# A streaming encoder step: rows of u at an even pace, ten single sets of v rows, and row requests three ahead

## The chip, the core and the metric

The kernel runs on one core of one Trainium2 chip. The metric is the device time of one execution in microseconds (us); the time before is the median of three runs. The engines are called as the profile calls them: PE (matmul), PEld (its weight load), DVE (vector), ACT (scalar), POOL (general purpose; it issues the gathers) and SP (it issues the weight transfers).

## The reference, cut to what matters

The model has two layers. Each ends in a PEER block: every token of the normed stream `xn` picks 128 experts (8 heads x 16) of 16,384, takes their rows `u` of a table (1,024 numbers each), multiplies them with its own `xn`, puts the sums through a gelu and a gate, and adds up the experts' rows `v` with these factors.

```python
eid = (e1 * PEER_NKEYS + e2).reshape(PEER_TOKEN_BLOCK, PEER_HEADS * PEER_TOPK)
ue = jnp.take(u_tab, eid, axis=0)
act = jax.nn.gelu(jnp.einsum('tkd,td->tk', ue, xb).astype(jnp.float32))
ve = jnp.take(v_tab, eid, axis=0)
return jnp.einsum('tk,tkd->td', (gate * act).astype(xb.dtype), ve)
```

There are 384 tokens: 256 of a prompt and 128 of running streams (the sample). All arithmetic is float32.

## The kernel before

The function `peer` (L924) does the block twice, once per layer. The prompt tokens are done densely: PE multiplies with the whole tables, 128 blocks of 128 experts each. The sample tokens are done sparsely, by gathered rows. Both run beside each other, and the sparse part is dealt out over the dense part by step numbers.

**Steps.** Steps 0 to 63 make the first half of the dense u products. Steps 64 to 127 (here the gates stage, loop at L1529) make the second half, and beside them the first half of the gates. Steps 128 to 255 (here the values stage, loop at L1564) multiply with the v blocks; up to about step 188 they also make the second half of the gates. A step of the values stage has on PE twelve matmuls (L179) or, in every fifth step of the first sixty, eight unsplit ones (L1436). The block arrives by SP as `raw` (512 KB); ACT makes `hi` (L130), DVE makes `lo` (L131) two steps before PE needs it, and DVE also makes `plo` of the activations. Every second step has a gate: DVE makes `ob`, `og` and half of `oa` (L1376 to L1394), PE takes them in sixteen short matmuls (L1403), DVE multiplies the result into `G` (L1409).

**Rows of u.** The 128 u rows of the sample are gathered by POOL (L1233), one row per partition, 128 x 1024 numbers, into a ring of three buffers `gath`, and DVE multiplies each with `xn` and sums it up (L1278, `u_item`). `U_DUE` (L61) gives how many rows shall be done before a step; between its pairs the rows are dealt out evenly (`tick`, L1450). The request for row k+2 stands in the program ahead of the product of row k. A request can go out when its buffer is free: with three buffers, when the product of row k-3 is done.

**Sets of v rows.** 96 of the 128 v rows are taken on PE in sets of four (`v_quad`, L1340, sixteen matmuls at L1348). `V_DUE` (L62) gives the step of each of the 24 sets: six in the gates stage, 18 in the values stage. In the values stage the rows lie in eight slots of `G[0]`, room for two sets, so the four gathers of a set wait until PE has taken the set two before it. The other 32 rows (`v_item`, L1298) are summed on DVE (L1303) in the steps between the two numbers of `I_DUE` (L59). The last gate is multiplied in at about step 188, and from step 192 on both halves of `G` are done with: the work on the sample fills what DVE has left. This last part of the values stage is what the title of the change calls phase 192.

**What sets the order.** PE, DVE and ACT keep the order in which the program is written through both stages (`in_order`, L85). POOL and SP do not: their order is the scheduler's. Each is a queue: a gather that waits holds back all gathers behind it. The extra buffers of the values stage (third `hi` and `lo`) lie in the pool `lpool` (L1558).

Of the kernel before, what the change touches and what calls it, by code (L numbers as in the profile page):

```python
# [9 lines left out]
F32 = mybir.dt.float32  # L10
F32R = mybir.dt.float32r
# [8 lines left out]
P = 128  # L20
D = 1024
KD = D // P
NB = 3
NP = 256
# [31 lines left out]

GD = 2
QR = [r for r in range(32) if r // RG != GD]
I_DUE = (192, 250)  # L59
AHEAD = 2 * 64 - 5  # L60
U_DUE = ((64, 22), (71, 27), (78, 33), (104, 53), (128, 72), (148, 87), (196, P))  # L61
V_DUE = ([82, 86, 90, 94, 98, 103] + [149 + 6 * i for i in range(7)] + [196 + 9 * (i // 2) for i in range(11)])  # L62
V_SLOTS = [(1, 36 + 4 * i, 66, 100 + 4 * i) for i in range(6)] + [(0, e, 128 + e + 5, 256) for e in (0, 4, 8, 12, 20, 24, 28, 32)]


# [1 line left out]
def encoder_step(ctx: ExitStack, tc: tile.TileContext, t_in, t_out):  # L67
# [4 lines left out]
    def T(pl, shape, dt=F32, tag=None, bufs=None):  # L72
        n_names[0] += 1
        return pl.tile(shape, dt, tag=tag, name=f"{tag}_{n_names[0]}", **({} if bufs is None else {"bufs": bufs}))
# [62 lines left out]
    more, turn_of = {}, {}  # L137
# [786 lines left out]
    def peer(l):  # L924
        with ExitStack() as c:
            one = c.enter_context(tc.tile_pool(name="p1", bufs=1))

            eidU = T(one, [P, GR, TG], I32, tag="eidU")
# [15 lines left out]
            gap = lambda n, i: T(qpool, [P, n // 4], F32, tag=f"gap{i}")  # L944
# [1 line left out]
            sync.dma_start(sk, t_in["sub_k"][l])  # L946
            gap(192, 0)
            qhi = T(qpool, [P, KD, NT], F32R, tag="qhi")
            gap(224, 1)
            qlo = T(qpool, [P, KD, NT], F32R, tag="qlo")  # L950
            gap(96, 2)
            qTp = T(qpool, [P, 2 * PH, NP], F32, tag="qTp")

            grow = G[0][:, HE - 4:].rearrange("p e t -> p (e t)")
# [6 lines left out]
            lpool = lent.__enter__()  # L961
# [268 lines left out]
            urows, vrows = {}, {}  # L1230

            def gather(tile_, tab, idx):
                pool.indirect_dma_start(out=tile_, out_offset=None, in_=tab,  # L1233
                                        in_offset=bass.IndirectOffsetOnAxis(ap=idx, axis=0))
                return tile_

            def fetch_u(k):
                if k < P:
                    g, j = divmod(k, TG)
                    urows[k] = gather(T(one, [P, D], F32, tag="gath", bufs=3), t_in["p_u"], eidU[:, g, j:j + 1])  # L1240

            def fetch_v(n, s):

# [6 lines left out]
            def v_slot(n, s):  # L1250
                return next((k for *k, s0, s1 in V_SLOTS if s0 <= s and V_DUE[n // 4] <= s1 and tuple(k) not in taken), None)

# [67 lines left out]
            def item_tick(s):  # L1320
                want = min(TG, max(0, TG * (s + 1 - I_DUE[0]) // (I_DUE[1] - I_DUE[0])))
                while done["i"] < want:
# [4 lines left out]
                    if done["i"] == TG:  # L1327
                        items_end()
                if s >= I_DUE[0] - 4:
                    fetch_item(s - 2 * HE)  # L1330
# [113 lines left out]
            done = {"u": 0, "v": 0, "f": 0, "i": 0, "g": 0, "c": 0}  # L1444
# [5 lines left out]
            def tick(s):  # L1450

                s0, n0 = start[0], 0
                for s1, n1 in U_DUE:
                    if s < s1:
                        break
                    s0, n0 = s1, n1
                want = P if s >= U_DUE[-1][0] else n0 + (n1 - n0) * (s + 1 - s0) // (s1 - s0)
                while done["u"] < want:
                    fetch_u(done["u"] + 2)
                    u_item(done["u"])  # L1460
                    done["u"] += 1

# [29 lines left out]
            for e2 in range(HE):  # L1492
                j = e2 - (HE - TURN)
                if j == 0:
                    more.clear()
                    lent.__exit__(None, None, None)
                    xfctx.__exit__(None, None, None)
                    xpool = tc.tile_pool(name="px", bufs=1, side="right")
                    xp = xpool.__enter__()
                    xhi = T(xp, [P, KD, NP], F32R, tag="xhi")  # L1500
                    T(xp, [P, 8], F32, tag="gap")
                    xlo = T(xp, [P, KD, NP], F32R, tag="xlo")
                u_gelu(e2, u_products(e2, u_weights(e2)))
                if j >= 0:
                    ks = slice(2 * (j // 2), 2 * (j // 2) + 2)
                    x_, q_ = ((xhi, qhi), (xlo, qlo))[j % 2]
                    pin(act.copy(x_[:, ks], q_[:, ks, :NP]))
                if busy:
                    busy = pull(sample, 2)
                    if not busy:  # L1510
                        start[0] = e2 + 1
                        fetch_u(0)
                        fetch_u(1)
                else:
                    pull(prompt, 2 if e2 % 4 == 0 else 1)
                    tick(e2)
# [41 lines left out]
            lpool = (lent := tc.tile_pool(name="pe1", bufs=1, side="right")).__enter__()  # L1558
            turn_of.pop("hi"), turn_of.pop("lo")
            turn_of.update(hi=1, lo=1)  # L1560
            more.update(hi=(lpool, 1), lo=(lpool, 1))
            stage = [(wt, ph)]
            n = 1
            for e2 in range(2 * HE):  # L1564
# [44 lines left out]
    peer(0)  # L1609
    attention()  # L1610
    peer(1)
    final()

# [95 lines left out]
```

## Time and profile before

| What | Value |
|---|---|
| runs | 2437.0, 2439.88, 2450.36 us; median 2439.88 |
| profiled execution | 2438.17 us; its span 2436.5 us |
| busy, share of the span | PE 96%, PEld 83%, DVE 81%, ACT 51%, POOL 31% |
| DMA | 649.76 MB, mean 267 GB/s |
| gates stage, layer 0 and 1 | 665.8 to 888.2 us and 1765.0 to 1991.1 us |
| values stage, layer 0 and 1 | 888.2 to about 1325 us and 1991.1 to about 2426 us |

The profile is of one execution. In a group of instructions the last column is the time that the engine stood idle just before them and what ended it. In the table by stretch of time each engine has its busy time in the stretch, so that the stretch less PE's busy time is PE's idle time; the columns behind POOL are the granted TensorE clock, the busy share of the DMA engines and GB/s. Step numbers are not in the trace: they are counted from the matmuls.

### The profile page before, as it was taken

To read this page: it belongs to the slowest core of one execution; us is meant where nothing else is said; L and a number is where in the kernel's file an instruction comes from. 1 tells how busy PE (TensorE), PEld (TensorE's weight loads), DVE (VectorE), ACT (ScalarE), POOL (GpSimd) and SP (SyncE) were. 2 spreads that over 40 slices of the span, in tenths; PEclk is the share of its full clock that TensorE was granted. 3 is DMA by queue.
4 is the path that set the end of the run, shared out by engine and by line. 5 is a ranking of instruction groups with operands and counts; after the bars stand their busy time and mean duration, and the time that the engine had idled before them with its cause. 6 is when DMAs were issued, how large, how long until landed. Compare 5 with 4: busy or idle time off the path is not lost.

```text
span 2436.5 us, 44422 instructions
## 1 busy us (share of the span) xinstructions
PE 2345.2 (96%) x16591; PEld 2011.4 (83%) x16592; DVE 1965.2 (81%) x4233; ACT 1249.7 (51%) x2428; POOL 747.7 (31%) x779
## 2 busy tenths in 40 slices
PE   7999999999999999899999998999999999999998
PEld 7899988999998987566776877999998997666776
DVE  5988846989998999787776675989997999787676
ACT  5656524434565666454444554344465666453443
POOL 2222200012245334455551100011244324454550
PEclk9999999999999999999999999999999999999999
DMA  5555434357799889999995424357799889999995
GB/s 198 176 187 179 155 134 159 136 211 247 254 336 365 307 299 335 354 381 352 415 393 170 139 71 166 126 212 250 247 343 340 308 298 332 372 374 349 413 400 182
DMA packets 177080, 649.76 MB, mean 267 GB/s; under 512 B 21136, under 2 KB 23040, under 8 KB 174208
## 3 DMA queue, kind: packets, MB, share of 16 engines
q1 hardware_dynamic: 99936, 365.85, 41.7%
q0 software_dynamic: 76928, 281.07, 31.1%
q8 instruction: 130, 2.13, 0.3%
q14 instruction: 86, 0.70, 0.1%
HBM read 630.62 MB, written 18.06 MB: 266 GB/s over the span
## 4 chain that ended last, share of the span: by engine, by line
PE 80%; DVE 7%; DMA 5%; issue 4%; ACT 3%; POOL 1%; another core or an unknown queue 0%; POOLq 0%; SPq 0%; ACTq 0%; DVEq 0%
PE bank L179 24%; PE bank L166 13%; PE bank L168 13%; PE bank L167 12%; DMA gath<-in_p_u,eidU 5%; PE bank L1348 3%; PE bank L1361 2%; PE bank L1403 2%; DVE lo L131 2%; PE bank L1436 2%; DVE gath L1278 1%; ACT hi L130 1%; PE bank L533 1%; PE bank L472 1%; PE bank L473 1%
## 5 line engine op out<-in xcount | busy, mean ns | idle before, releaser
L130 ACT CAST hi<-raw 128x1024 fp32r<-128x1024 f32 (+1 forms) x476 | 495.4, 1041 | 728.8 <-PE bank L167 324.2
L131 DVE TENSOR_TENSOR lo<-raw,hi 128x1024 fp32r<-128x1024 f32 (+1 forms) x476 | 575.7, 1210 | 193.8 <-ACT hi L130 166.2
L1233 POOL DMA_INDIRECT gath<-in_p_u,eidU x256 | 323.8, 1265 | 863.8 <-DVE gath L1278 516.8
L166 PE MATMUL bank<-xhi,hi 128*128 128x256 f32 (+1 forms) x1344 | 407.1, 303 | 0.9 <-issue 0.9
L168 PE MATMUL bank<-xhi,lo 128*128 128x256 f32 (+1 forms) x1344 | 398.0, 296 | 9.4 <-DVE lo L131 8.2
L167 PE MATMUL bank<-xlo,hi 128*128 128x256 f32 (+1 forms) x1344 | 398.4, 296 | 0.0
L168 PEld LDWEIGHTS bank<-xhi,lo 128*128 128x128 f32 x1344 | 255.2, 190 | 14.9 <-DVE lo L131 12.9
L166 PEld LDWEIGHTS bank<-xhi,hi 128*128 128x128 f32 x1344 | 253.9, 189 | 16.1 <-issue 8.7
L1233 POOL DMA_INDIRECT G<-in_p_v,eidT x192 | 213.7, 1113 | 141.1 <-PE bank L1348 76.1
L167 PEld LDWEIGHTS bank<-xlo,hi 128*128 128x128 f32 x1344 | 255.5, 190 | 0.4
L166 PE MATMUL bank<-qhi,hi 128*128 128x256 f32 (+1 forms) x784 | 232.9, 297 | 0.0
L168 PE MATMUL bank<-qhi,lo 128*128 128x256 f32 (+1 forms) x784 | 228.6, 292 | 2.0 <-DVE lo L131 2.0
L167 PE MATMUL bank<-qlo,hi 128*128 128x256 f32 (+1 forms) x784 | 229.6, 293 | 0.0
L179 PE MATMUL bank<-lo,phi 128*128 128x512 f32 x632 | 198.5, 395 | 9.2 <-DVE lo L131 9.0
L1391 ACT ACTIVATE oa<-ioh,e2T 128x128 f16<-128x128 f16 x512 | 163.3, 390 | 84.5 <-PE bank L1403 80.0
L179 PE MATMUL bank<-hi,phi 128*128 128x512 f32 x632 | 205.5, 406 | 0.2
L130 ACT CAST hix<-raw 128x1024 fp32r<-128x1024 f32 x118 | 123.7, 1048 | 152.1 <-PE bank L167 70.2
L179 PE MATMUL bank<-hi,plo 128*128 128x512 f32 x632 | 196.2, 392 | 0.0
L1278 DVE SCALAR_TENSOR_TENSOR gath<-gath,G 128x1024 f32<-128x1024 f32 x128 | 155.9, 1218 | 36.6 <-DMA gath<-in_p_u,eidU 33.2
L1278 DVE SCALAR_TENSOR_TENSOR gath<-gath,xg 128x1024 f32<-128x1024 f32 x128 | 155.5, 1216 | 9.2 <-DMA gath<-in_p_u,eidU 9.2
L131 DVE TENSOR_TENSOR lox<-raw,hix 128x1024 fp32r<-128x1024 f32 x118 | 143.7, 1218 | 22.2 <-ACT hix L130 19.2
L179 PEld LDWEIGHTS bank<-hi,phi 128*128 128x128 f32 x632 | 115.0, 189 | 44.2 <-issue 18.7
(391 smaller groups left out, 5120.9 us busy)
## 6 DMA issues: line engine op xcount, KB each, us to landing
raw<-in_u_t SPq DMA_DIRECT2D x256, 512.0 KB
raw<-in_p_v SPq DMA_DIRECT2D x256, 512.0 KB
raw<-in_w_in SPq DMA_DIRECT2D x32, 512.0 KB
raw<-in_p_w_q SPq DMA_DIRECT2D x32, 512.0 KB
raw<-in_w_z SPq DMA_DIRECT2D x16, 512.0 KB
s<-in_state_ssm SPq DMA_DIRECT2D x8, 1024.0 KB
out_sm_ssm<-s SPq DMA_DIRECT2D x8, 1024.0 KB
raw<-in_w_out SPq DMA_DIRECT2D x16, 512.0 KB
```

The source lines that it names most:

```text
L130: act.copy(hi, raw)
L131: dve.tensor_tensor(lo, raw, hi32, op=OP.subtract)
L166: pe.matmul(ps, whi[:, s], xhi[:, k, c0:c1], start=(k == 0), stop=False)
L167: pe.matmul(ps, whi[:, s], xlo[:, k, c0:c1], start=False, stop=False)
L168: pe.matmul(ps, wlo[:, s], xhi[:, k, c0:c1], start=False, stop=(k == KD - 1))
L179: mm = pe.matmul(ps, x, w[:, hf * n:(hf + 1) * n], start=s_, stop=e_)
L1233: pool.indirect_dma_start(out=tile_, out_offset=None, in_=tab, in_offset=bass.IndirectOffsetOnAxis(ap=idx, axis=0))
L1278: pin(dve.scalar_tensor_tensor(tile_, tile_, 1.0, xg[g], op0=OP.mult, op1=OP.mult, accum_out=au[g][:, j:j + 1]))
L1348: pe.matmul(out_s[hf][32 * q:32 * q + 32, :], cm[:, q], rows[q][:, hf * 512:hf * 512 + 512], start=(r == 0), stop=False, tile_position=(0, ...
L1361: pe.matmul(ps, wt[0][:, k * P:(k + 1) * P], xf[:, k], start=(k == 0), stop=(k == KD - 1))
L1391: act.activation(a[:, i], ioh, AF.Square, scale=-1.0, bias=e2T[:, t, 0:1])
L1403: pe.matmul(ps[:, i], ones[i // 4][:, i % 4], eg[:, i, j], start=(j == 0), stop=(j == 1))
```

## The change

Three tables and one buffer change; no arithmetic does.

- `U_DUE`: 46 rows in the gates stage (50 before), 47 in steps 128 to 191 (52 before), and the last 13 in steps 192 to 202, more than one a step. All 128 are done after step 202 (195 before).
- `V_DUE`: the sets six steps apart go on to step 203 (ten of them; seven before). The last eight come in pairs at 207, 218, 229 and 240. Before, eleven came from 196 to 241, in pairs nine steps apart but for the last.
- `I_DUE`: the 32 rows on DVE are dealt out over steps 203 to 249, not 192 to 249.
- In the values stage every fourth u row (k % 4 = 3) gets a buffer of its own, `gathx`, in `lpool`, and the request for row k+3 stands ahead of the product of row k. A request then waits for the product of row k-4. The gaps between `qhi`, `qlo`, `qTp` and between `xhi`, `xlo` are moved so that the pools still fit.

```diff
-I_DUE = (192, 250)
+I_DUE = (203, 250)
 AHEAD = 2 * 64 - 5
-U_DUE = ((64, 22), (71, 27), (78, 33), (104, 53), (128, 72), (148, 87), (196, P))
-V_DUE = ([82, 86, 90, 94, 98, 103] + [149 + 6 * i for i in range(7)] + [196 + 9 * (i // 2) for i in range(11)])
+U_DUE = ((64, 22), (128, 68), (192, 115), (203, P))
+V_DUE = ([82, 86, 90, 94, 98, 103] + [149 + 6 * i for i in range(10)] + [207 + 11 * (i // 2) for i in range(8)])
...
             qhi = T(qpool, [P, KD, NT], F32R, tag="qhi")
-            gap(224, 1)
             qlo = T(qpool, [P, KD, NT], F32R, tag="qlo")
-            gap(96, 2)
+            gap(64, 1)
             qTp = T(qpool, [P, 2 * PH, NP], F32, tag="qTp")
...
             def fetch_u(k):
                 if k < P:
                     g, j = divmod(k, TG)
-                    urows[k] = gather(T(one, [P, D], F32, tag="gath", bufs=3), t_in["p_u"], eidU[:, g, j:j + 1])
+                    extra = k % 4 == 3 and k >= more.get("u", P)
+                    tile_ = T(lpool, [P, D], F32, tag="gathx", bufs=1) if extra else T(one, [P, D], F32, tag="gath", bufs=3)
+                    urows[k] = gather(tile_, t_in["p_u"], eidU[:, g, j:j + 1])
...
                 while done["u"] < want:
-                    fetch_u(done["u"] + 2)
+                    fetch_u(done["u"] + 2 + ("u" in more))
                     u_item(done["u"])
...
                     xhi = T(xp, [P, KD, NP], F32R, tag="xhi")
+                    xlo = T(xp, [P, KD, NP], F32R, tag="xlo")
                     T(xp, [P, 8], F32, tag="gap")
-                    xlo = T(xp, [P, KD, NP], F32R, tag="xlo")
...
-            more.update(hi=(lpool, 1), lo=(lpool, 1))
+            more.update(hi=(lpool, 1), lo=(lpool, 1), u=done["u"] + 2)
+            fetch_u(more["u"])
```

What it does to the queues is seen at three places, all in layer 0 (layer 1 reads alike). The lines of kernel.py are one or two off between the two versions. The first is POOL's queue at the four gathers that wait for the set of step 185. In the names, `gath` and `gathx` are buffers of u rows, `eidT` stands in gathers for a set, `eidU` with `G` in gathers for DVE's rows. Before, the u row right behind the four (gath_13071, row 121) is due in step 188:

```order
L1233 DMA gath_13036<-in_p_u,eidU_3964 128x1024
L1233 DMA G_626_3975<-in_p_v,eidT_3971 128x1024 x4
L1233 DMA gath_13071<-in_p_u,eidU_3964 128x1024
L1233 DMA G_626_3975<-in_p_v,eidU_3964 128x1024
L1233 DMA gath_13110<-in_p_u,eidU_3964 128x1024
L1233 DMA gath_13153<-in_p_u,eidU_3964 128x1024
```

And now, where the row behind the same four is row 113 (gath_13045), due in step 190:

```order
L1232 DMA gath_13010<-in_p_u,eidU_3964 128x1024
L1232 DMA G_626_3975<-in_p_v,eidT_3971 128x1024 x4
L1232 DMA gath_13045<-in_p_u,eidU_3964 128x1024
L1232 DMA G_626_3975<-in_p_v,eidU_3964 128x1024
L1232 DMA gath_13084<-in_p_u,eidU_3964 128x1024
L1232 DMA gathx_13150<-in_p_u,eidU_3964 128x1024
```

The four gathers stand where they stood; the u rows around them are eight lower in number, and each is due two steps later than the one that stood there.

The second place is the same queue farther on. Before, from the last three u rows on (rows 125 to 127):

```order
L1233 DMA gath_13229<-in_p_u,eidU_3964 128x1024
L1233 DMA gath_13254<-in_p_u,eidU_3964 128x1024
L1233 DMA gath_13279<-in_p_u,eidU_3964 128x1024
L1233 DMA G_626_3975<-in_p_v,eidU_3964 128x1024
L1233 DMA G_626_3975<-in_p_v,eidT_3971 128x1024 x7
```

And now, from the four gathers that wait for the set of step 191, with the u rows 118 (gath_13237) to 126 behind them:

```order
L1232 DMA G_626_3975<-in_p_v,eidT_3971 128x1024 x4
L1232 DMA gath_13237<-in_p_u,eidU_3964 128x1024
L1232 DMA gathx_13263<-in_p_u,eidU_3964 128x1024
L1232 DMA gath_13289<-in_p_u,eidU_3964 128x1024
L1232 DMA gath_13314<-in_p_u,eidU_3964 128x1024
L1232 DMA gath_13341<-in_p_u,eidU_3964 128x1024
L1232 DMA gathx_13375<-in_p_u,eidU_3964 128x1024
L1232 DMA G_626_3975<-in_p_v,eidT_3971 128x1024 x3
L1232 DMA gath_13378<-in_p_u,eidU_3964 128x1024
L1232 DMA G_626_3975<-in_p_v,eidT_3971 128x1024
L1232 DMA gath_13404<-in_p_u,eidU_3964 128x1024
L1232 DMA gath_13430<-in_p_u,eidU_3964 128x1024
```

Ten u rows now stand behind the gathers of step 191's set, and the last four of them behind those that wait for the set of step 197 (row 124, gath_13378, is due in step 200).

The third place is DVE's order at the end of the u rows. `lo` and `plo` belong to the dense part, `cm` to the sets (L1335) or to the end of a group of u rows (L1285). Before, steps 194 and 195:

```order
L131 TENSOR_TENSOR lo_13287<-raw_13284,hi_13286 128x1024
L131 TENSOR_TENSOR plo_13291<-G_1211_7476,phi_13290 128x256
L1278 SCALAR_TENSOR_TENSOR gath_13254,au_12007<-gath_13254,G_626_3975 128x1024
L131 TENSOR_TENSOR lo_13310<-raw_13307,hi_13309 128x1024
L131 TENSOR_TENSOR plo_13314<-G_1211_7476,phi_13313 128x256
L1335 SCALAR_TENSOR_TENSOR cm_13329<-ioh_74,a_10448 128x128
L1335 SCALAR_TENSOR_TENSOR cm_13331<-ioh_74,a_10448 128x128
L1278 SCALAR_TENSOR_TENSOR gath_13279,au_12007<-gath_13279,G_626_3975 128x1024
L1285 TENSOR_TENSOR cm_13334<-au_12007,same_q_86 128x128
L1303 SCALAR_TENSOR_TENSOR G_626_3975<-G_626_3975,cU_3966 128x1024
```

And now, from row 124 in step 200 to the last in step 202:

```order
L1279 SCALAR_TENSOR_TENSOR gath_13378,au_12307<-gath_13378,G_626_3975 128x1024
L131 TENSOR_TENSOR lo_13464<-raw_13461,hi_13463 128x1024
L131 TENSOR_TENSOR plo_13468<-G_1210_7475,phi_13467 128x256
L1279 SCALAR_TENSOR_TENSOR gath_13404,au_12307<-gath_13404,G_626_3975 128x1024
L131 TENSOR_TENSOR lox_13488<-raw_13485,hix_13487 128x1024
L131 TENSOR_TENSOR plo_13492<-G_1210_7475,phi_13491 128x256
L1336 SCALAR_TENSOR_TENSOR cm_13507<-ioh_74,a_10668 128x128
L1279 SCALAR_TENSOR_TENSOR gath_13430,au_12307<-gath_13430,G_626_3975 128x1024
L1279 SCALAR_TENSOR_TENSOR gathx_13457,au_12307<-gathx_13457,G_626_3975 128x1024
L1286 TENSOR_TENSOR cm_13511<-au_12307,same_q_86 128x128
```

The group ends seven steps later, and its last products stand closer to each other, with a `lo` that PE needs between them.

## The prediction

> **What bounds the kernel now.** I read the page first, then the busy time by stretch, the waits in the stretches that lose, and the order of events at the worst of them. The page's span, its chain of work, and one line of its list of transfers:
>
> ```profile
> span 2436.5 us, 44422 instructions
> PE 80%; DVE 7%; DMA 5%; issue 4%; ACT 3%; POOL 1%; another core or an unknown queue 0%; POOLq 0%; SPq 0%; ACTq 0%; DVEq 0%
> raw<-in_p_v SPq DMA_DIRECT2D x256, 512.0 KB
> ```
>
> PE carries 80% of the chain, so a change that leaves PE's work alone, as this one does, can win only what PE waits or runs at a lower clock. Where that is shows in the table by stretch (length; busy time of PE, PEld, DVE, ACT, POOL; granted clock; DMA share; GB/s), layer 0 and then layer 1:
>
> ```profile
> core 0: us, PE busy (x) PEld busy (x) DVE busy (x) ACT busy (x) POOL busy (x), PEclk, DMA share, GB/s
> 665.80:888.20 222.40, 218.42 (x2162) 204.67 (x2161) 196.06 (x302) 143.35 (x292) 92.48 (x81) 1.00 0.91 330
> 951.90:1110.00 158.10, 149.32 (x910) 98.95 (x908) 131.65 (x229) 81.81 (x171) 82.31 (x72) 0.97 0.96 365
> 1110.00:1126.00 16.00, 13.01 (x58) 10.26 (x58) 11.66 (x18) 6.53 (x10) 6.92 (x6) 0.79 1.02 392
> 1126.00:1307.00 181.00, 180.83 (x892) 135.28 (x891) 133.71 (x171) 76.96 (x115) 78.40 (x65) 1.00 0.92 357
> ...
> 1765.00:1991.10 226.10, 219.87 (x2162) 206.21 (x2161) 196.25 (x302) 143.33 (x292) 91.17 (x81) 0.99 0.91 325
> 2054.80:2212.00 157.20, 148.40 (x932) 99.89 (x931) 133.40 (x231) 83.35 (x173) 83.02 (x73) 0.99 0.98 372
> 2212.00:2226.00 14.00, 8.55 (x32) 6.65 (x31) 7.71 (x12) 3.32 (x6) 4.62 (x4) 0.88 0.87 335
> 2226.00:2408.00 182.00, 181.87 (x896) 136.07 (x895) 135.73 (x175) 78.32 (x117) 81.43 (x66) 1.00 0.92 360
> ```
>
> The rows of 158.1 and 157.2 us (steps 150 to 188 or so) I call A. There PE idles 158.10 − 149.32 = 8.78 us, and the clock of 0.97 costs 0.03 × 158.1 = 4.7 more: 13.5 us. In layer 1 it is 8.80 + 0.01 × 157.2 = 10.4, so A loses 23.9 us. The short rows behind them (to step 192) I call B: 2.99 + 0.21 × 16 = 6.4 and 5.45 + 0.12 × 14 = 7.1, together 13.5 us. The rows from step 192 on idle 0.17 and 0.13 us: nothing can be won there, only lost. The gates stage idles 3.98 us, and in layer 1 6.23 + 0.01 × 226.1 = 8.5.
>
> What PE waits for, by the table of waits (engine and line waited with; us in total, times, longest): A and B of layer 0, then of layer 1:
>
> ```profile
> DVE gath L1278 <- DMA gath<-in_p_u,eidU: 14.1, 7, 6.2
> PE bank L1403 <- DVE og L1379: 8.6, 5, 4.3
> ...
> DVE gath L1278 <- DMA gath<-in_p_u,eidU: 4.1, 1, 4.1
> PE bank L179 <- DVE lo L131: 3.0, 1, 3.0
> ...
> DVE gath L1278 <- DMA gath<-in_p_u,eidU: 13.8, 7, 4.7
> PE bank L1403 <- DVE og L1379: 7.2, 4, 3.9
> ...
> DVE gath L1278 <- DMA gath<-in_p_u,eidU: 6.3, 1, 6.3
> PE bank L179 <- DVE lo L131: 5.4, 1, 5.4
> ```
>
> PE waits for DVE, and DVE waits for a u row; DVE keeps its written order, so `og` and `lo` stand behind the product that waits. Why the row is late shows at B, in order of time (start, length, engine, operation):
>
> ```profile
> 1100.78 0.99 POOL L1233 DMA_INDIRECT G<-in_p_v,eidT  x1 [0.36 <-issue]
> 1106.41 0.94 POOL L1233 DMA_INDIRECT gath<-in_p_u,eidU  x1 [0.30 <-issue]
> 1116.63 1.22 DVE L1278 SCALAR_TENSOR_TENSOR gath<-gath,G 128x1024 f32<-128x1024 f32 x1 [4.10 <-DMA gath<-in_p_u,eidU]
> ...
> 2200.80 1.03 POOL L1233 DMA_INDIRECT G<-in_p_v,eidT  x1 [0.31 <-issue]
> 2219.07 1.22 DVE L1278 SCALAR_TENSOR_TENSOR gath<-gath,G 128x1024 f32<-128x1024 f32 x1 [6.29 <-DMA gath<-in_p_u,eidU]
> ```
>
> The first request of the four for a set goes out at 1100.78, when PE has taken the set of step 185. Row 121 stands fifth in the queue and can be multiplied at 1116.63: 15.9 us after the burst began, 18.3 in layer 1. The program wants it three steps behind the set. What a step lasts, by the chain (start, length, what):
>
> ```profile
> 1168.41 3.57 PE bank L1348 x32
> 1171.99 24.70 PE bank L179 x108
> ```
>
> Twelve matmuls take 24.70 × 12 / 108 = 2.74 us, and a set of sixteen 3.57 / 2 = 1.79.
>
> **The change part by part.** *A: the new numbers of `U_DUE`.* The row behind each burst is now due two steps later (row 113 instead of 121 in the order shown): 5.5 us. DVE's longest waits in A are 6.2 and 4.7 us, PE's 4.3 and 3.9. So PE's waits for `og` go, and the stalls with them that lowered the clock. Bounds: the 23.9 us all go, or only half goes, if the rows, spread more evenly, meet the bursts in other places. I leave 1.5 us per layer for a last late gate and take a gain of 23.9 − 3.0 = 20.9. DVE, which could be next, is not full in A (131.65 of 158.10 us) and has five u products fewer before step 192.
>
> *Fourth buffer, requests three ahead.* It does nothing for the row right behind a burst, since POOL's queue is in order and the four gathers wait for PE. It lets the rows ahead of a burst be asked for earlier, so I count nothing. The cover is that queue; without it a row would come up to one product earlier.
>
> *The moved gaps and `gathx` in `lpool`.* The first `gathx` row is asked for at the entry of the values stage, and none can start before `xpool` is closed. What hides this is the dense product of step 127. If that cover were gone it would cost one wait like those of A, 4.3 us per layer. I take nothing.
>
> *Gates stage.* Four u rows fewer, at an even pace of 46 in 64 steps. Durations of DVE's operations, grouped over 888 to 1125 us (count, busy time, mean ns, idle before):
>
> ```profile
> L131 DVE TENSOR_TENSOR lo<-raw,hi 128x1024 fp32r<-128x1024 f32 x35 | 42.6, 1216 | 0.1
> L1278 DVE SCALAR_TENSOR_TENSOR gath<-gath,G 128x1024 f32<-128x1024 f32 x28 | 34.1, 1219 | 14.1 <-DMA gath<-in_p_u,eidU 13.9
> L131 DVE TENSOR_TENSOR plo<-G,phi 128x256 fp32r<-128x256 f32 x54 | 22.5, 417 | 0.0
> ```
>
> 4 × 1.22 = 5 us less of DVE per layer, where PE idles 4 to 8 us. The gain lies between −1 (rows that now meet other work) and +4. I take 1 us per layer, near the lower end, since DVE has 26 us to spare there as it is: a gain of 2.
>
> *B and what replaces it.* The waits of B go, as in A. Behind step 191's set the row is due in step 195: one step more and a set between, 2.74 + 1.79 = 4.5 us later than the row in B. B's stalls on PE were 3.0 and 5.4: nothing is left in layer 0, 1 us in layer 1. Behind step 197's set row 124 is due in step 200, three steps as in B, but DVE has no slack now. In steps 192 to 202 it has eleven `lo` and `plo` and thirteen products: 11 × (1.22 + 0.42) + 13 × 1.22 = 33.9 us, beside PE's 11 × 2.74 + 2 × 1.79 = 33.7. Queued behind the waiting product on DVE are the `lo` of two steps, and PE waits for those. Bounds: 0, if the row lands a step sooner, to 5.4 as in layer 1's B. I take 3.0 in layer 0 and 4.5 in layer 1. The clock: B lost 3.4 us by it in layer 0 and 1.7 in layer 1, so 2.5 each, the mean.
>
> The Trainium skill says in "TensorE: Matmul & The Clock Gate", Part 1, that the clock halves after at least one idle window of some 3.4 us. By that layer 0's stall of 3.0 would cost no clock, and my sum would be 2.5 us less; the trace speaks against it, since B's longest wait there was 3.0 us and the granted clock still 0.79.
>
> *The pair at step 207.* Its second set's rows can be asked for when step 203's set is done. Until PE wants them there are four steps and the pair's first set: 4 × 2.74 + 1.79 = 12.7 us. Five transfers took 15.9, so four take between 15.9 × 4/5 = 12.7 and 15.9: a wait of 0 to 3. I take 1 per layer. The pairs behind it are eleven steps apart, two more than before, and didn't wait then.
>
> So B's 13.5 become 3.0 + 2.5 + 1 = 6.5 and 1 + 4.5 + 2.5 + 1 = 9.0, together 15.5: a loss of 2.0.
>
> *Sum.* The profiled execution took 2438.17 us, 1.7 more than its span and 1.7 less than the median of 2439.88. 2438.17 − 20.9 − 2 + 2.0 = 2417.3, which by the median would be 2419.0. I say 2418.
>
> **The rivals.** *All hidden.* The row behind step 197's set comes in time: then A's 20.9, B's 13.5 and the gates' 2 are won, 36.4 us: 2439.88 − 36.4 = 2403.5, and with half of the 3.0 us that I left in A, 2402. For it: the tail from step 192 had 47 us of DVE to spare (181.0 − 133.7), and with four buffers a row can be asked for one product sooner. Against it: thirteen products in eleven steps.
>
> *The loss moves, and isn't removed.* The new dense stretch takes two stalls of 7 us (4.5 and the clock's 2.5) in each layer, behind step 191's set and behind 197's, and the pair's 1: 28 + 2 = 30 where B had 13.5. Or A's rows come no sooner than before because the queue decides, which would leave a like sum. 2439.88 − 20.9 − 2 + 16.5 = 2433.5, no change. For it: DVE is full there, and a late `lo` can't be made up for. Against: two of the eleven steps have a set, which gives DVE time.
>
> *The tail at the mean rate.* From step 192 to 250 come 58 weight blocks, 10 u rows, 36 rows of sets and 26 of DVE's 32, 130 transfers of 0.524 MB (128 x 1024 numbers; 512 KB): 68.2 MB. PE needs 58 × 2.74 + 10 × 1.79 = 176.8 us, so 386 GB/s are wanted, where 124 transfers were wanted before and 357 and 360 GB/s moved. At 358 they last 190.5 us, 13.7 longer, in each layer: 2439.88 − 36.4 + 27.4 = 2430.9, no change. It speaks against it that the transfers moved so little because PE wanted no more; the rate by stretch at 1175 to 1200 us:
>
> ```profile
> 1175.00:1200.00 25.00, 25.00 (x128) 18.58 (x126) 19.69 (x25) 12.17 (x18) 12.20 (x11) 1.00 1.02 417
> ```
>
> The Trainium skill names this as a limit: "DMA: Bandwidth & Descriptors" gives about 358 GB/s from HBM per core; the trace differs, with 417 GB/s here.
>
> *Slower: the transfers become the bound.* Gathers and weights together fall to the 335 GB/s of the row from 2212.00. Then 68.2 MB last 203.6 us, 26.8 longer than PE needs, in both layers: 2439.88 − 36.4 + 53.6 = 2457. It decides below 339 GB/s. For it: row requests now stand closer, and the DMA share is 0.96 to 1.02 in three rows. Against: the 417, and that PE was waiting during the 335.
>
> **How the numbers follow.** The forecast has 0.50, all hidden 0.20, the moved loss 0.15, the mean rate 0.07, the transfers as the bound 0.08. What a measurement of this kernel can tell from no change is about 0.5%, 12.2 us: faster is below 2427.7, slower above 2452.1. The forecast's own bounds (stalls of 0 to 5.4, clock, pair 0 to 3, gates −1 to +4, half of A's gain) reach from 2408 to 2428. Faster: 0.50 + 0.20 and 0.02 from the good end of the moved loss, 0.72; same: its other 0.13 and 0.07, 0.20; slower 0.08. The range goes from all hidden at 2402 to the moved loss at 2434; the slower case and the ends beyond are left out.
>
> **What would show it.** Right: PE's idle time and clock loss in A fall from 23.9 to a few us; DVE's waits for `gath` before step 188 stay under 2 us each; one wait of PE for `lo` of 2 to 5 us about step 200, and a granted clock under 0.9 there. Wrong: waits of `og` in A as long as before (the two steps don't help); no stall from 192 to 207 (all hidden); stalls behind both sets (the loss moved); or PE waiting for `hi` or `raw` from step 203 on with less than 360 GB/s (the transfers).

## The result and the profile after

The changed kernel took 2421.36 us (median of four runs, 2420.12 to 2425.08), beside 2442.99 for the kernel before, measured with it. The ratio is 0.9919, with an interval of 0.9896 to 0.9942. A second measurement gave 0.9908 (0.9880 to 0.9937). So the change gains 0.8 to 0.9%, as was forecast (2418 to 2439.88 is 0.9910). But the parts of the sum came out otherwise than forecast, and the experiments found that the buffer without the new tables gains more than twice as much.

The profiled execution took 2425.08 us, the slowest of the four. Its span, busy times and chain of work:

```profile
span 2423.4 us, 44427 instructions
PE 2321.5 (96%) x16591; PEld 1991.9 (82%) x16592; DVE 1964.2 (81%) x4233; ACT 1250.2 (52%) x2428; POOL 768.1 (32%) x779
PE 79%; DVE 9%; DMA 4%; issue 3%; ACT 2%; another core or an unknown queue 1%; POOL 1%; SPq 0%; POOLq 0%; DVEq 0%; ACTq 0%
```

The table by stretch, cut at the same steps in both layers: gates stage; steps 148 to 188 (the A of the prediction); 189 to 191; 192 to 203; 204 to 249. Columns: length; busy time of PE, PEld, DVE, ACT, POOL; granted clock; DMA share; GB/s.

```profile
663.95:888.83 224.88, 214.59 (x2162) 201.16 (x2161) 191.60 (x294) 143.47 (x292) 88.12 (x78) 0.98 0.88 318
952.50:1096.90 144.40, 144.40 (x925) 97.95 (x923) 128.46 (x221) 83.02 (x173) 81.20 (x66) 1.00 1.00 386
1096.90:1107.20 10.30, 10.30 (x60) 7.15 (x56) 8.27 (x15) 5.17 (x8) 6.76 (x5) 1.00 1.02 414
1107.20:1154.30 47.10, 39.79 (x181) 28.42 (x177) 32.97 (x51) 16.27 (x24) 23.72 (x18) 0.93 0.96 372
1154.30:1299.00 144.70, 144.15 (x709) 108.44 (x705) 112.00 (x140) 60.54 (x91) 72.05 (x55) 1.00 0.93 365
1756.80:1982.86 226.06, 214.32 (x2163) 201.17 (x2161) 191.73 (x294) 143.45 (x292) 88.24 (x77) 0.98 0.88 316
2046.50:2191.00 144.50, 144.50 (x926) 98.06 (x924) 128.21 (x221) 83.18 (x173) 80.53 (x67) 1.00 1.00 384
2201.20:2248.50 47.30, 38.61 (x181) 27.84 (x177) 32.83 (x51) 16.28 (x24) 24.20 (x19) 0.96 0.96 377
```

Before, the stretches 148 to 188 and 192 to 203, layer 0 and layer 1:

```profile
951.90:1110.50 158.60, 149.82 (x926) 99.45 (x924) 132.15 (x229) 82.31 (x171) 82.69 (x72) 0.97 0.96 365
1124.10:1162.80 38.70, 38.53 (x185) 29.30 (x184) 29.46 (x42) 16.26 (x25) 17.23 (x16) 0.98 0.90 339
2054.80:2210.50 155.70, 146.90 (x926) 98.64 (x924) 131.90 (x229) 82.60 (x172) 82.46 (x72) 0.99 0.98 371
2225.80:2263.70 37.90, 37.77 (x186) 28.74 (x185) 29.99 (x44) 16.26 (x25) 19.45 (x16) 1.00 0.92 352
```

A has no loss left: PE is busy for the whole 144.40 and 144.50 us at full clock, where before the same steps took 158.6 and 155.7. The loss now sits in steps 192 to 203: 47.10 − 39.79 = 7.3 us of idle time and 0.07 × 47.1 = 3.3 of clock in layer 0, 8.7 and 1.9 in layer 1. What is waited for there, from the table of waits, first layer 0, then layer 1:

```profile
DVE gath L1279 <- DMA gath<-in_p_u,eidU: 14.5, 5, 7.1
PE bank L1349 <- DVE cm L1336: 6.7, 2, 4.8
PE bank L179 <- DVE lo L131: 0.6, 1, 0.6
...
DVE gath L1279 <- DMA gath<-in_p_u,eidU: 14.8, 5, 7.2
PE bank L1349 <- DVE cm L1336: 7.1, 2, 5.7
PE bank L179 <- DVE lo L131: 1.6, 1, 1.6
```

It is the old chain in a new place: PE waits for DVE (here for `cm`, the factors of a set), DVE for a row of u. In order of time, behind the set of step 191:

```profile
1107.48 1.74 POOL L1232 DMA_INDIRECT G<-in_p_v,eidT  x1 [1.56 <-PE bank L1349]
1113.68 1.55 POOL L1232 DMA_INDIRECT gath<-in_p_u,eidU  x1 [0.30 <-issue]
1125.65 1.23 DVE L1279 SCALAR_TENSOR_TENSOR gath<-gath,G 128x1024 f32<-128x1024 f32 x1 [7.13 <-DMA gath<-in_p_u,eidU]
1128.61 3.64 PE L1349 MATMUL bank<-G,cm 128*32 128x512 f32 x16 [4.80 <-DVE cm L1336]
```

DVE was ready for the row at 1125.65 − 7.13 = 1118.5, 11.0 us after the burst's first request, and got it after 18.2. The set behind it took 3.64 us instead of 1.8: PE had waited 4.80 us and ran at the lower clock.

There is a loss after step 250 that the forecast didn't have. DVE's order at the end has the sums into `h` (L1597) ahead of a `lo` that PE needs:

```profile
1304.77 1.28 DVE L1597 TENSOR_TENSOR h<-h,bank 128x512 f32<-128x512 f32 x2 [6.21 <-PE bank L179]
1305.97 1.22 DVE L131 TENSOR_TENSOR lo<-raw,hi 128x1024 fp32r<-128x1024 f32 x1
```

In the waits of this stretch PE pays 2.1 us for it in layer 0 (and as much in layer 1, where it was 0.2 before):

```profile
PE bank L179 <- DVE lo L131: 2.1, 1, 2.1
```

Before, that `lo` stood ahead of the sums (L1595 there):

```profile
1311.61 1.22 DVE L131 TENSOR_TENSOR lo<-raw,hi 128x1024 fp32r<-128x1024 f32 x1 [4.73 <-ACT hi L130]
1313.71 1.28 DVE L1595 TENSOR_TENSOR h<-h,bank 128x512 f32<-128x512 f32 x2 [0.54 <-DMA h<-hd]
```

The sums lie behind the stretch whose order is fixed, so here the scheduler chose. From step 250 to the next layer the changed kernel takes 49.9 us instead of 46.4, and in layer 1 30.4 instead of 28.2.

Put together from the two profiles, by the starts of the steps on PE (layer 0 and layer 1, in us):

| Stretch | Before | After | Forecast of the difference | Measured |
|---|---|---|---|---|
| A, 148 to 188 | 158.6, 155.7 | 144.5, 144.5 | −20.9 | −25.3 |
| 189 to 249 (B, the dense rows, the pairs) | 196.9, 197.8 | 202.0, 202.1 | +2.0 | +9.4 |
| gates stage | 222.4, 226.1 | 224.9, 226.1 | −2.0 | +2.5 |
| after 250 | 46.4, 28.2 | 49.9, 30.4 | 0 | +5.7 |
| all else | | | 0 | −5.4 |
| span | 2436.5 | 2423.4 | −20.9 | −13.1 |

"After 250" runs to the next layer's first matmul, in layer 1 to the end. Between 189 and 249 both kernels have eleven sets, so the numbers can be compared directly.

### The profile page after: what moved, and what is told of

It reads as the page before. It is cut to its first block, busy times and chain, and to the rows that moved or that the text cites. A ratio compares the mean times of both kernels' runs of the same rounds, so it can differ in the third digit from the quotient of the medians.

```text
span 2423.4 us, 44427 instructions
## 1 busy us (share of the span) xinstructions
PE 2321.5 (96%) x16591; PEld 1991.9 (82%) x16592; DVE 1964.2 (81%) x4233; ACT 1250.2 (52%) x2428; POOL 768.1 (32%) x779
## 4 chain that ended last, share of the span: by engine, by line
PE 79%; DVE 9%; DMA 4%; issue 3%; ACT 2%; another core or an unknown queue 1%; POOL 1%; SPq 0%; POOLq 0%; DVEq 0%; ACTq 0%
PE bank L179 26%; PE bank L166 11%; PE bank L168 11%; PE bank L167 11%; PE bank L1349 4%; PE bank L1437 3%; DVE lo L131 3%; DMA gath<-in_p_u,eidU 3%; PE bank L1404 2%; PE bank L1362 2%; ACT hi L130 1%; DVE gath L1279 1%; PE bank L533 1%; PE bank L472 1%
## 5 line engine op out<-in xcount | busy, mean ns | idle before, releaser
L1232 POOL DMA_INDIRECT gath<-in_p_u,eidU x226 | 279.7, 1238 | 779.3 <-DVE gath L1279 443.0
L1232 POOL DMA_INDIRECT G<-in_p_v,eidT x192 | 236.7, 1233 | 155.6 <-PE bank L1349 98.4
L166 PEld LDWEIGHTS bank<-xhi,hi 128*128 128x128 f32 x1344 | 255.7, 190 | 15.6 <-issue 7.8
L1279 DVE SCALAR_TENSOR_TENSOR gath<-gath,G 128x1024 f32<-128x1024 f32 x112 | 136.4, 1219 | 37.2 <-DMA gath<-in_p_u,eidU 37.2
L168 PEld LDWEIGHTS bank<-qhi,lo 128*128 128x128 f32 x784 | 148.1, 189 | 2.8 <-DVE lo L131 2.8
L167 PEld LDWEIGHTS bank<-qlo,hi 128*128 128x128 f32 x784 | 148.8, 190 | 0.4
```

The source lines that it names most:

```text
L166: pe.matmul(ps, whi[:, s], xhi[:, k, c0:c1], start=(k == 0), stop=False)
L167: pe.matmul(ps, whi[:, s], xlo[:, k, c0:c1], start=False, stop=False)
L168: pe.matmul(ps, wlo[:, s], xhi[:, k, c0:c1], start=False, stop=(k == KD - 1))
L1279: pin(dve.scalar_tensor_tensor(tile_, tile_, 1.0, xg[g], op0=OP.mult, op1=OP.mult, accum_out=au[g][:, j:j + 1]))
```

## The experiments

Each ran beside the kernel before on one chip, and the ratio to that is what is compared. A burst is the four gathers of one set. "Reached" is the time from a burst's first request to the moment when DVE is ready for the row behind it (start of the product less its wait). The moved gaps stay in every run, so no run shows what they are worth by themselves.

**The tables without the buffer.**

```diff
-                    extra = k % 4 == 3 and k >= more.get("u", P)
+                    extra = False
-                    fetch_u(done["u"] + 2 + ("u" in more))
+                    fetch_u(done["u"] + 2)
-            more.update(hi=(lpool, 1), lo=(lpool, 1), u=done["u"] + 2)
-            fetch_u(more["u"])
+            more.update(hi=(lpool, 1), lo=(lpool, 1))
```

> The new tables with three buffers and requests two rows ahead, as before. Theory 1 (queue and tables): the row right behind a burst of four set gathers decides, POOL's queue is in order, so a fourth buffer moves it little: steps 148 to 189 stay at 144.4 to 146 us per layer, PE's stall at the set of step 197 stays at 4 to 7 us, the time is within 3 us of the changed kernel's 2421. Theory 2 (the buffer carries the gain): A's waits for og come back, steps 148 to 189 take 150 us or more, the time is 2432 or more. Theory 3 (transfers): fewer rows in flight let the row behind step 191's set land sooner, 15 us instead of 18.2 after the burst's first request; the stall shrinks by 2 to 3 us a layer, 2415 to 2418.

It took 0.9955 of before (0.9939 to 0.9971). Steps 148 to 188 and 189 to 203:

```profile
945.00:1090.10 145.10, 144.56 (x924) 98.00 (x923) 128.49 (x221) 83.16 (x173) 79.86 (x66) 1.00 1.00 381
1090.10:1153.20 63.10, 52.09 (x235) 37.87 (x231) 41.78 (x68) 21.44 (x32) 32.56 (x24) 0.92 0.94 362
2036.10:2181.10 145.00, 144.67 (x926) 98.05 (x924) 128.88 (x222) 82.94 (x172) 79.43 (x67) 1.00 0.99 381
2181.10:2243.40 62.30, 51.70 (x234) 37.62 (x230) 40.06 (x65) 21.68 (x32) 31.34 (x24) 0.92 0.95 367
```

A is all but empty here too (145.2 and 145.0 us), so the tables do this alone, as theory 1 had it; theory 2's waits for `og` did not come back. But in steps 189 to 191 PE waits 1.7 and 2.2 us for a set's `cm`, and steps 192 to 203 take 51.1 and 49.8 us, with two stalls of about 4 to 5 us in each layer. Row 116, behind three gathers of step 191's burst, came after 13.4 and 12.8 us, sooner, as theory 3 had it; but DVE was there after 7.0 and 6.3, so the stalls didn't shrink. The buffer on top of the tables is thus worth some 0.4% (the interval overlaps that of the first measurement of the changed kernel, not that of the second), behind step 188 and not in A.

**The buffer without the tables.** The old `U_DUE`, `V_DUE` and `I_DUE` stand in the changed kernel.

```diff
-I_DUE = (203, 250)
+I_DUE = (192, 250)
-U_DUE = ((64, 22), (128, 68), (192, 115), (203, P))
+U_DUE = ((64, 22), (71, 27), (78, 33), (104, 53), (128, 72), (148, 87), (196, P))
-V_DUE = ([82, 86, 90, 94, 98, 103] + [149 + 6 * i for i in range(10)] + [207 + 11 * (i // 2) for i in range(8)])
+V_DUE = ([82, 86, 90, 94, 98, 103] + [149 + 6 * i for i in range(7)] + [196 + 9 * (i // 2) for i in range(11)])
```

> The fourth buffer and requests three ahead with the old tables. Theory 1: no change from before beyond 4 us, 2437 to 2443; the stall near step 188 stays, since the burst holds the row back and not the buffer. Theory 2: the waits for og of steps 150 to 188 go, 2420 to 2428. Theory 3: more in flight makes bursts land later, 2443 or more.

2390.4 us, 0.9808 of before (0.9795 to 0.9821): more than twice the whole change's gain. Theory 1, which expected no change, fell, and theory 2's range of 2420 to 2428 was passed by 30 us. Stretches of steps 148 to 188, 189 to 203 and 204 to 249 in this kernel, layer 0 and layer 1:

```profile
948.80:1093.40 144.60, 144.59 (x926) 98.03 (x924) 131.50 (x228) 83.07 (x172) 84.94 (x72) 1.00 1.01 400
1093.40:1140.20 46.80, 45.77 (x227) 35.66 (x224) 41.03 (x59) 20.52 (x31) 23.66 (x20) 1.00 0.97 382
1140.20:1284.50 144.30, 144.30 (x713) 107.60 (x711) 104.48 (x130) 62.53 (x92) 57.61 (x50) 1.00 0.93 364
2029.50:2173.90 144.40, 144.40 (x925) 97.97 (x924) 131.87 (x228) 83.26 (x173) 85.62 (x71) 1.00 1.01 400
2173.90:2220.90 47.00, 46.29 (x227) 35.49 (x224) 40.59 (x59) 20.23 (x31) 24.10 (x20) 1.00 0.98 381
```

Of 336 us in layer 0 PE idles about one. Not all of the gain is explained by this: in the two profiles A gives 25.3 us and steps 189 to 249 give 12.1, of 43.2 in all. The gates stage gives 7.6 more (220.5 and 220.4 us), and there no row uses the new buffer; whether that is the moved gaps or the execution, no run shows. At the place of the old B, in order of time:

```profile
1083.90 1.04 POOL L1232 DMA_INDIRECT G<-in_p_v,eidT  x1 [0.30 <-issue]
1089.60 0.93 POOL L1232 DMA_INDIRECT gath<-in_p_u,eidU  x1 [0.30 <-issue]
1100.31 1.22 DVE L1279 SCALAR_TENSOR_TENSOR gath<-gath,G 128x1024 f32<-128x1024 f32 x1
```

The row behind the burst is now row 122, where before it was row 121. One more row went ahead of the four gathers, so DVE comes to the one behind them 16.4 us after the first request (11.7 before), and by then it is there. A row that is late need not cost PE anything: behind step 179's set DVE waits 3.7 us here, and PE doesn't idle.

**The rows at one pace to step 203.**

```diff
-U_DUE = ((64, 22), (128, 68), (192, 115), (203, P))
+U_DUE = ((64, 22), (128, 68), (203, P))
```

> The u rows at one pace from step 128 to 203 (60 rows in 75 steps, 0.80 a step, instead of 0.73 and then 1.18). Theory 1: what counts is how long DVE takes to reach the row behind a burst. In the changed kernel that is some 20 us before step 186 and 11.0 behind step 191's set, where the row needs 18.2. At 0.80 a step it would be about 18 and 15: A stays without stalls of 2 us, the stall of PE at the set of step 197 falls from 5.0 and 5.9 us to 0 to 2 and takes its clock loss along, 2404 to 2412. Theory 3 (transfers): the rows land as late as DVE reaches them later, nothing is won: 2418 to 2424. A rival: A's old waits come back at 0.80 (before it had 0.75 and 0.85): 148 to 189 over 149 us a layer, 2420 or more.

2403.9 us, 0.9866 (0.9849 to 0.9883): the good end of theory 1's range. A stayed empty, and 189 to 203 took 49.2 and 51.8 us instead of 57.3 and 57.5. The way there was not quite as theory 1 had it. The row behind step 191's set was reached after 13.6 us, near the 15 expected, but it came after 20.6, so DVE still waited 7.0. PE's wait was short (1.8 and 2.6 us), since here the factors of the set (`cm`) stood ahead of the late product in DVE's order, and not behind it:

```profile
1111.43 0.28 DVE L1336 SCALAR_TENSOR_TENSOR cm<-ioh,a 128x128 f32<-128x128 f16 x1
1118.68 1.23 DVE L1279 SCALAR_TENSOR_TENSOR gath<-gath,G 128x1024 f32<-128x1024 f32 x1 [6.96 <-DMA gath<-in_p_u,eidU]
```

The last row, 127, stands behind step 197's set, was reached after 11.4 us and waited for 5.5 and 6.0. In layer 0 this cost PE a wait of 1.3 us behind step 204 and a granted clock of 0.81 over 9 us.

**Half the weight blocks left out.** Of the fourteen blocks of steps 192 to 205 in each layer, seven are not loaded; the block before is multiplied again in their place.

```diff
+                if 64 <= e2 < 78:
+                    if e2 % 2 == 0:
+                        last_raw[:] = [load_raw(vtab[e2])]
+                    return split_raw(last_raw[0])
                 return load_split(vtab[e2])
```

> The changed kernel, but the weight blocks of steps 193, 195 and so on to 205 aren't loaded: the block before is split and multiplied again, so seven transfers of 512 KB per layer are left out there and part of the computation is another. Theory 1 (queue): burst, issue and row stay as they are; the row behind step 191's set can be multiplied 16 us or more after the burst's first request (18.2 in the changed kernel), DVE's wait stays at 5 to 7 us. Theory 3 (transfers): the row lands 11 to 13 us after the first request, DVE's wait falls below 2.5 us and PE's stall at step 197 below 1; 2404 to 2412.

2397.1 us, 0.9834 (0.9820 to 0.9849), below the range of theory 3. Behind step 191's set, the burst, the row's request and its product:

```profile
1103.79 0.94 POOL L1232 DMA_INDIRECT G<-in_p_v,eidT  x1 [0.30 <-issue]
1110.28 1.98 POOL L1232 DMA_INDIRECT gath<-in_p_u,eidU  x1 [0.30 <-issue]
1117.64 1.22 DVE L1279 SCALAR_TENSOR_TENSOR gath<-gath,G 128x1024 f32<-128x1024 f32 x1 [3.25 <-DMA gath<-in_p_u,eidU]
```

The request comes as late as in the changed kernel (6.5 us after the first, there 6.2), but the row is there 7.4 us after it instead of 12.0. So about 4 of DVE's 7.1 us of waiting come from the transfers that were left out. The 3.3 that stay are the queue, the row's due step and whatever the other transfers still cost; no run separates these. The row came 13.9 us after the first request and PE waited 1.7 and 0.5 us at step 197's set: nearer to theory 3 than to theory 1, and outside the numbers of both. How full the transfers were while the row was under way (DMA share and GB/s at the end), in the changed kernel and here:

```profile
1113.70:1125.70 12.00, 10.12 (x45) 8.05 (x43) 4.87 (x9) 6.05 (x10) 5.63 (x4) 1.00 1.03 420
1110.30:1117.60 7.30, 7.30 (x34) 6.05 (x33) 4.09 (x6) 4.05 (x6) 5.23 (x4) 1.00 0.98 354
```

So behind a burst the DMA engines were full or nearly so in both, also in the changed kernel, where steps 192 to 203 as a whole moved only 372 GB/s.

**The changed kernel again, on one chip with three of the runs that follow.**

> The changed kernel itself once more, beside the others on one chip. The gates stage took 224.9 and 226.1 us in its first profile, and 215 to 220 in two kernels that have the same rows up to step 128. Theory 1 (that was the execution, not the tables): 216 to 221 here, time 0.985 to 0.990 of before. Theory 2 (the chip or the tables): 224 or more again, 0.990 or more. Both expect PE's stalls at step 197 (5 to 6 us) and behind step 197's set (2 us and some) again.

0.9908 (0.9880 to 0.9937). Its gates stage, layer 0 and layer 1:

```profile
666.60:886.30 219.70, 211.84 (x2163) 200.13 (x2162) 191.56 (x294) 143.37 (x292) 92.28 (x77) 0.98 0.89 325
1753.10:1970.80 217.70, 212.07 (x2163) 200.19 (x2162) 191.59 (x294) 143.34 (x292) 91.09 (x78) 0.98 0.89 328
```

The same program took 224.9 and 226.1 us there in its first profile. So one profile cannot tell what the gates' new numbers are worth. More can be said by all that came after: the four profiles with these numbers (tables only, even to 203, half the blocks, this one) take 215.4 to 219.7 us a layer, 218.0 in the mean, and the four with the old ones (buffer only, two ahead, and the next two runs) 218.3 to 220.7, 219.8 in the mean. PE's stalls behind the late bursts are back (192 to 203: 46.0 and 46.4 us).

**The old u rows beside the new sets.**

```diff
-U_DUE = ((64, 22), (128, 68), (192, 115), (203, P))
+U_DUE = ((64, 22), (71, 27), (78, 33), (104, 53), (128, 72), (148, 87), (196, P))
```

> The changed kernel with the old U_DUE: rows done after step 195, the new V_DUE and I_DUE and the fourth buffer stay. One row, the last, still stands behind the set gathers of step 191. Theory 1 (the rows of u behind the late bursts cost, not the sets): two stalls per layer become one, of 4 to 8 us with its clock; steps 189 to 204 take 50 to 54 us instead of 57.4; 0.984 to 0.988 of before. Theory 2 (the ten single sets, the pairs eleven steps apart and the denser end cost): 189 to 204 and what follows step 204 stay as in the changed kernel, 0.989 or more.

0.9910 (0.9884 to 0.9936), with 57.9 and 55.8 us for steps 189 to 203, near theory 2. But what is waited for is one row: row 127, the only one behind step 191's set, was reached after 11.2 and 12.3 us and came after 18.8 and 19.5. With the stall's length misjudged, this run could not separate row and sets; the next one was made to.

**The same, with the last row ahead of that burst.**

```diff
-U_DUE = (..., (148, 87), (196, P))
+U_DUE = (..., (148, 87), (194, P))
```

> As the kernel with the old U_DUE beside the new V_DUE and I_DUE, but the last pair of U_DUE is (194, P), two steps earlier, so that the last row is requested ahead of step 191's set gathers and no row of u stands behind them; the sets stay as they are. Theory 1 (one row behind one burst makes the stall): PE doesn't wait at step 197, steps 189 to 204 take 48 to 50 us (with three sets) instead of 57.9 and 55.8, the time falls to 0.982 to 0.985 of before. Theory 2 (the sets six steps apart after step 188, or the fuller transfers, cost by themselves): 55 us or more, 0.989 or more.

0.9912 (0.9889 to 0.9935): the time is as theory 2 had it. But the stretches show that its reason is another. Steps 148 to 188, 189 to 191 and 192 to 203 of layer 0:

```profile
945.50:1095.60 150.10, 146.19 (x924) 98.35 (x923) 134.31 (x233) 83.19 (x173) 85.64 (x72) 0.99 1.00 389
1095.60:1111.40 15.80, 11.78 (x59) 7.29 (x55) 9.88 (x17) 5.17 (x8) 6.06 (x5) 0.89 1.02 405
1111.40:1149.20 37.80, 37.80 (x188) 28.61 (x184) 22.73 (x35) 16.36 (x25) 8.83 (x8) 1.00 0.82 288
```

With no row of u behind it, step 191's burst stalls nothing: steps 192 to 203, with the single sets of 197 and 203, run without a gap. So these sets don't stall PE by themselves, at least not with the 288 GB/s that are moved there once the u rows are done. But at 0.89 rows a step DVE is too soon at bursts before: row 123, behind step 185's set, was reached after 13.3 and 14.3 us, DVE waited 5.9 and 5.7, and PE 4 to 5. The same happened in A, behind step 161's set: row 102 was reached after 10.7 us, DVE waited 5.1 and 5.6 and PE 3.9 and 4.2, where the kernel with the buffer alone reaches its row 102 after 13.8 and 14.0. The stall had moved to earlier bursts.

**The buffer with requests two ahead.** In the kernel with the buffer alone, the requests stand two rows ahead in the program as before.

```diff
-                    fetch_u(done["u"] + 2 + ("u" in more))
+                    fetch_u(done["u"] + 2)
-            fetch_u(more["u"])
```

> The fourth buffer with the old tables, but requests two rows ahead as before. Theory 1 (the buffer lets one more row pass ahead of each burst; where the request stands in the program matters not, since POOL's order is the scheduler's): as with requests three ahead, 0.979 to 0.983 of before, no stall of PE from step 148 to 189. Theory 2 (the request three ahead does it): between, 0.988 or more, waits for og again.

2388.9 us, 0.9809 (0.9781 to 0.9836): theory 1. The row behind step 185's set is 122 here too. It is the buffer that lets it be, not the place of the request.

**The buffer with even gates, and with two even paces.** First `U_DUE` = ((64, 22), (128, 72), (148, 87), (196, P)), then ((64, 22), (128, 71), (196, P)), both with the old `V_DUE` and `I_DUE`.

> The fourth buffer with the old tables, but the 50 rows of the gates stage at one pace (72 done at step 128 as before). Theory 1 (an even pace helps the gates stage a little): the gates stage takes 1 to 3 us less per layer than the 220.5 of the kernel with the buffer alone, 0.977 to 0.981 of before. Rival: the pace there is nothing, or the bumps were there for a reason: the same or up to 3 us longer, 0.981 to 0.984.

> The fourth buffer with the old V_DUE and I_DUE and u rows at two even paces: 71 done at step 128, all at 196. Theory 1: as with the even gates alone (2386.9), 0.977 to 0.983 of before, no wait of PE for og in steps 148 to 189. Rival: 0.82 a step ahead of step 148 and behind it makes the rows behind the bursts late again, 0.985 or more.

2386.9 us, 0.9803 (0.9778 to 0.9828), and 2393.9 us, 0.9834 (0.9808 to 0.9860). The even gates stage took 216.8 and 220.3 us, beside 218.3 and 218.7 in the kernel with requests two ahead on the same chip, so the first run decides nothing. The second lies between its theory and its rival; PE's longest wait for `og` in A was 0.4 us. The three that have the buffer and 72 rows done by step 128 can't be told apart from each other, and all beat the changed kernel clearly.

## Why the forecast held, point by point

The rows behind the bursts, worked out for each kernel as above (layer 0 / layer 1, us; the last column is steps 189 to 249, all with eleven sets; with the tables only, row 116 stands behind three of the four gathers):

| Kernel | Behind step 185: row, reached, DVE's wait | Behind step 191: row, reached, DVE's wait | 189 to 249 |
|---|---|---|---|
| before | 121, 11.7 / 12.0, 4.1 / 6.3 | none | 196.9 / 197.8 |
| changed | 113, 15.5 / 16.9, 0 / 0 | 118, 11.0 / 11.8, 7.1 / 7.2 | 202.0 / 202.1 |
| tables only | 112, 12.3 / 13.4, 4.5 / 4.0 | 116, 7.0 / 6.3, 6.4 / 6.5 | 207.0 / 207.0 |
| buffer only | 122, 16.4 / 16.3, 0 / 0.3 | none | 191.2 / 191.4 |
| even to 203 | 117, 15.6 / 15.6, 1.5 / 3.3 | 122, 13.6 / 13.7, 7.0 / 6.3 | 196.1 / 196.1 |
| old u rows | 122, 15.6 / 16.6, 0.6 / 0 | 127, 11.2 / 12.3, 7.6 / 7.3 | 200.7 / 198.6 |
| rows end at 194 | 123, 13.3 / 14.3, 5.9 / 5.7 | none | 196.4 / 198.3 |

- *What bounds the kernel* was right: a row of u behind four set gathers in POOL's queue holds DVE, and DVE holds PE. Every wait in the table is of this kind, and so is A's longest stall before: behind step 161's set DVE reached row 101 after 9.0 us and waited 6.2, where the changed kernel reaches its row there after 18.4 and doesn't wait.
- *A* was right and a little larger: 25.3 us instead of 20.9. Nothing of it was left, where the forecast had left 3.0.
- *The fourth buffer at nothing* was the wrong step: "It does nothing for the row right behind a burst, since POOL's queue is in order". The queue is in order, but which row stands behind the burst isn't fixed. With one more buffer one more row is ahead of it, and DVE reaches the next one row later. The two steps that the prediction gave to `U_DUE` alone were one of the tables and one of the buffer: behind step 185's set stands row 112 with the tables only and row 113 with both. Either alone empties A (the tables only leave 1.7 and 2.2 us of stall in steps 189 to 191), and with both the second has nothing left to win there.
- *The row behind step 191's set* was mis-sized: nothing and 1 us were forecast for PE, and 4.8 and 5.7 came. "One step more and a set between, 4.5 us later" fails twice. B's three steps had a gate and unsplit matmuls among them: it took DVE 11.7 us from the burst's first request to the row, and the four steps here take 11.0. And the set of step 197 comes after the row is used, not before. So DVE reaches the row no later than in B (11.0 and 11.8 us), and it comes later, after 18.2 and 19.0 us. The transfers have a share in that, as the run with half the blocks shows: at least 4 us of 7.
- *Behind step 197's set* DVE waited 4.1 and 5.0 us for row 124, and PE lost less than the 3.0 and 4.5 forecast: 6.7 + 0.6 − 4.8 = 2.5 and 7.1 + 1.6 − 5.7 = 3.0 us. Most of it was a wait for `cm` and not for `lo`. *The clock*, 2.5 a layer: 3.3 and 1.9.
- *The pair at 207*, 1 us a layer: the wait at its second set cost 0.2 and 0.7 us (the pair took 3.85 and 4.31 us, other pairs 3.64). Steps 204 to 249 take as long as before with one set of 1.8 us less, but they also hold eight short matmuls that end the group of u rows (L1261, 0.8 us), which before lay ahead of step 204. So they lost about 1.0 us a layer in all, and the size was right.
- *The gates stage* stays open: the program's own executions differ by 5 and 8 us there, more than the 2 in question. The means of the later profiles, 218.0 and 219.8 a layer, point to a gain of 1.8 a layer beside the forecast's 1, but the two ranges overlap and the profiles are of three chips.
- *After step 250*, not in the sum: 5.7 us. All seven profiles with the new `V_DUE` and `I_DUE` take 47.3 to 50.4 and 30.0 to 32.1 us there, all four with the buffer and the old ones 45.8 to 46.6 and 28.0 to 28.5. The changed kernel's trace names the wait (`lo` behind `h`, 2.1 us in each layer, and in layer 0 the clock besides); an undoing of that order wasn't tried.
- *The rivals.* The transfers didn't become the bound of a whole stretch, nor did a mean rate of 358, though behind step 191's burst they had their share: in steps 192 to 249 PE waited for no `hi` and no `raw`, and 372 and 377 GB/s moved where it lost most. The moved loss came in part: its sign, stalls behind both sets, is there, and steps 189 to 249 cost 9.4 us more than before, between the forecast's 2.0 and that rival's 16.5. The new `U_DUE` beside the old sets wasn't tried, so which table costs how much is known only in part.
- *The sum.* Steps 189 to 249, the gates and the end came out 7.4, 4.5 and 5.7 us worse than forecast, A and the rest of the program 4.4 and 5.4 better, so the two profiles differ by 13.1 us and not by 20.9. What made the rest 5.4 us shorter, no run shows. The medians differ by 21.6, since the profiled execution after is 3.7 us above its median and the one before 4.8 below. That the median came so close to 2418 is in part luck: errors of 17.6 us one way and 9.8 the other, and then the choice of the profiled executions, made up for each other.

The Trainium skill gives in "DMA: Bandwidth & Descriptors", section Bandwidth, about 358 GB/s for a core when both cores of a pair stream, and up to 425 for one core alone. This kernel runs on one core, and the trace agrees with the second: with the buffer alone it moved 400 GB/s for 144 us in each layer. The Trainium skill also states, in "TensorE: Matmul & The Clock Gate", Part 1, that the clock halves after an idle window of about 3.4 us. Here the 7 us that hold the wait of 2.1 us behind `h` had a granted clock of 0.76:

```profile
1305.00:1312.00 7.00, 4.94 (x15) 3.79 (x15) 4.31 (x8) 3.32 (x7) 1.58 (x1) 0.76 0.26 76
```

So here a shorter wait cost clock too, in this case 0.24 × 7 = 1.7 us. Not every one does: the wait of 1.9 us at the set of step 203 left the granted clock at 1.00 from 1146 to 1155 us.

## What to carry to other kernels

When a transfer is late in a queue that is kept in order, ask which request stands behind the one that waits, and how long its consumer takes to come to it; one more buffer shifts that by a whole request. A deadline counted in steps has to be turned into time with the steps of that place, and with what stands between really ahead of the use. And if a change has several parts that cure the same wait, try each alone: here the kernel with the buffer and the old tables takes 0.9808 of the time, and the new tables gave more than half of that gain back.

## What had not been expected of the hardware

Where DVE waited, the row right behind three or four gathers of a set came 12.3 to 20.6 us after the first of them was requested. With seven of fourteen weight blocks left out, the row itself took 7.4 us from its request instead of 12.0, and while it was under way with the full load, 420 GB/s were moved, where the stretch as a whole has 372. And two executions of one program differ by 5 and 8 us in the gates stage, while its steps 148 to 188 repeat to 0.1 us.
